# Value weights' raws and query tables in free ring tiles, two weight splits behind the exponentials, latents' splits in other heads

## The chip, the cores and the metric

The kernel runs on one core of a Trainium2 chip. The time is the device time of one execution in microseconds (us); of several executions the median is given. Everything is computed in 32-bit floating point; a matrix product is made of three passes (high part by high part, high by low, low by high) over operands that are split into a rounded high part and a rest.

## The reference, cut to what matters

One denoising step of a two-layer backbone on 512 latent tokens and 128 prompt tokens, with 128 cached tokens. The even layer joins 8 heads of latent attention (MLA) and 8 heads of neighbourhood attention; the change touches the end of the neighbourhood heads and the start of the MLA heads.

```python
def even_mixer_latent(h, c_ckv, c_krope, c_nk, c_nv, w_in, q_norm, w_uq, kv_norm, w_ukv, rpb, w_out, cos, sin):
    q, ckv, krope, nq, nk, nv = even_project(h, w_in, q_norm, w_uq, kv_norm, w_ukv)
    q = jnp.concatenate([q[..., :MLA_NOPE_DIM], apply_rope(q[..., MLA_NOPE_DIM:], cos, sin)], axis=-1)
    krope = apply_rope(krope[:, :, None, :], cos, sin)[:, :, 0, :]
    k_lat, v_lat = mla_expand(ckv, w_ukv, krope)
    k_ctx, v_ctx = mla_expand(c_ckv, w_ukv, c_krope)
    a_mla = attend_blocked(q, jnp.concatenate([k_lat, k_ctx], axis=1),
                           jnp.concatenate([v_lat, v_ctx], axis=1), MLA_SCALE)
    a_na = neighbourhood_attention(nq, nk, nv, c_nk, c_nv, rpb)
    return jnp.concatenate([a_mla.reshape(b, L, -1), a_na.reshape(b, L, -1)], axis=-1) @ w_out
```

## The kernel before, in words

The order of each engine's instructions is fixed when the program is built: the code names pieces of TensorE's work in strings (`NA_ORDER`, L963, for the neighbourhood heads 0 to 7), `sequence` (L121) runs them in that order, and a scheduler places the instructions of the other engines; `after(inst, fn)` and `issue_after` put what `fn` issues on an engine behind `inst` on that engine. Every engine works through its own instructions in order, so one that waits holds all behind it. SyncE (SP) issues nearly all DMAs, in order too.

In the heads, `s` are scores, `t` transposes of the probabilities, `v` products with values, `q` the next pair's query or key projection, `m` modulation products, `sp`, `pt`, `pv` the prompt's part, and `pk` the place of a split of latents. Of the scores (`ns`), VectorE (DVE) adds the bias and takes the extreme (`np`, `nm`, the ISA rows), ScalarE (ACT) takes the exponential, GpSimd (POOL) scales it. Transposes (`nt`) are split into `nts_..h` by a copy of ACT and `nts_..l` by a subtraction of DVE, and then multiply the values into `no`. Score banks in PSUM come from a pool `y` of four.

`unit` (L170) loads a weight tile into one of three raw buffers (`rawp`), and splits it by a copy of ACT and a subtraction of DVE or POOL. `wna` (L709) does so for the query and key weights of the neighbourhood heads, pair by pair: `wnq2` and `wnq3` are the query weights of pairs 2 and 3, split one pair ahead. `split_in_place` (L863) splits the compressed latents `ckv`, `cq`, `kr`, `cc` in place, one entry of `SPLIT_AT` (L878) in each of heads 0 to 5, behind that head's second exponential. `moved` and `latents` (L883, L893) copy low parts and prompt columns into ring tiles by DMA (`ckv0l`, `ckph`, `ckpl`, `cq0l`). The ring holds eight tiles of each of the tags `x`, `hh` and `hl`; when head 6 begins its end, the eight `hh` tiles with the high parts of the layer's input have had their last reader.

Behind head 6's pieces the code takes the first MLA weights `wm0` (L1002), the latents, key tiles `kT`, and the value weights `wmv` (L1008). `k_pieces` and `q_pieces` (L930, L944) make MLA keys and queries; a query is multiplied by a rotation table `tq`, which head 7 loads for MLA head 0 into a raw buffer, and which is loaded again for all heads, two rows, when the neighbourhood pool is closed (L1030).

Of the kernel before, what the change touches and what calls it, by code (L numbers as in the profile page):

```python
# [51 lines left out]
def body(ctx, tc, xT, vecs, crow, wm0, wm0g1, wm0g, wm1, wA, wNV, wNA, wMK, wMV, wOA, wGQ, wGK, wGV, wOC,  # L52
# [53 lines left out]
    def f(ap):  # L106
        return ap.bitcast(F32)
# [62 lines left out]
    def unit(src, n, name, lo="v", pool=None, bufs=3):  # L170

        raw = load(src, n, name + "r")
        t = (pool or wp).tile([P, 2, 1024], F32R, tag="w", bufs=bufs, name=name)
        hi, lw = t[:, 0, :n], t[:, 1, :n]
        S.activation(hi, raw, AF.Copy)
        (V if lo == "v" else G).tensor_tensor(lw, raw, f(hi), ALU.subtract)
        return hi, lw
# [538 lines left out]

# [120 lines left out]

    wmk, nexps = {}, {}  # L840
# [32 lines left out]
    def cached_latents():  # L873
# [1 line left out]
        nc.sync.dma_start(cc, cckvT.rearrange("u p n -> p u n"))  # L875
        split_in_place("cc", cc, [("u", 0, 256)])
    HALVES = [("u", 0, HT), ("u", HT, T)]
    SPLIT_AT = [lambda: split_in_place("ckv0", ckv[0], [("t", 0, T)]),  # L878
                lambda: split_in_place("ckv1", ckv[1], [("t", 0, T)]), lambda: split_in_place("cq0", cq[0], HALVES),
                lambda: split_in_place("cq1", cq[1], HALVES), lambda: split_in_place("kr", kr, [("t", 0, T), ("u", T, 768)]),  # L880
                cached_latents]

    def moved(name):  # L883

# [82 lines left out]
    for h in range(8):  # L967
        p, r = divmod(h, 2)
        if r == 0:
            oN.append(ring.tile([P, T], F32, tag="x", name=f"oN{p}"))  # L970
            pfirst, psecond = prompt_pair([nv[4][:, 2 * p + i, :] for i in range(2)], oN[p], ab, f"npp{p}",
                                         lambda name: bank(name, "y"))
        pts = []
        sc = na_scores(h, bm, pts)
        if h < 7:
            bm = na_bias(h + 1)
        qh, ql, ks = [t[r] for t in nqk[p]]
        pieces = named("s", sc)
        if h < 6:
            pieces["pk"] = lambda h=h: after(nexps[h, 1], SPLIT_AT[h])  # L980

        def prompt_scores(pss, qh=qh, ql=ql, ks=ks):
            PE.matmul(pss, qh[:, NS:T], ks[:, 896:1024], start=True, stop=False)
            PE.matmul(pss, ql[:, NS:T], ks[:, 896:1024], start=False, stop=True)
        pieces["sp"] = pfirst(r, prompt_scores)
        if p < 3:
            pieces.update(named("q", na_q(p + 1) if r == 0 else na_k(p + 1)))
        for n, at in enumerate(M_AT):
            if h == at:
                pieces.update(named("n" if "m0" in pieces else "m", mod0(4 + n, lambda n=n: bank(f"mod{4 + n}", "y"),  # L990
                                                                               mod_raw_w if h == 6 else mod_raw)))
        if h == 7:
            cql = after(fetched["wmvr"], lambda: [moved(f"cq{u}") for u in range(2)])
            pieces.update(k_pieces(0, ybank))
            pieces.update(named("u", q_pieces(0, ybank, lambda c: ring.tile([P, T], F32R, tag="h" + c, name=f"mq{c}0"),
                                              lazy(lambda: load(tabM[:, 0, :], T, "tq0")))))
        sequence(NA_ORDER[h] if h else "q0 q1 s0 m0 q2 s1 sp pk q3 q4 q5 m1 q6 q7 m2", {**pieces, **tail})
        tail = na_values(h, pts, oN[p])
        if r == 1:
            tail.update(psecond)  # L1000
        if h == 6:
            mla_w(0)  # L1002
            lat = latents()
            kT = [[ring.tile([P, T], F32R, tag="h" + c, name=f"kT{c}{r}") for r in range(2)] for c in "hl"]
            kTp = ring.tile([P, T], F32R, tag="x", name="kTp")
            even_keys, first_odd = [[(kT[i][r], kTp[:, P * (2 * i + r):P * (2 * i + r + 1)]) for i in range(2)] for r in range(2)]
            odd_keys = [first_odd]
            wmv = unit(wMV, 1024, "wmv")  # L1008
        if h == 7:
            with tc.issue_after(fetched["cq1"].ins):  # L1010
                for r in range(2):
                    k_rope(r, (slice(64, 128), slice(0, 64))[r])
# [14 lines left out]

    sb = ExitStack()
    cp = sb.enter_context(tc.tile_pool(name="cp", bufs=1, reuse_waits="tile"))
    tq = cp.tile([P, 2, T], F32, name="tq")  # L1030
    nc.sync.dma_start(tq, tabM)
    mv = [cp.tile([P, 8, P], F32R, name=f"mv{i}") for i in range(6)]
    odd_keys.append([(cp.tile([P, T], F32R, name=f"kTo{c}"), cp.tile([P, P], F32R, name=f"kTq{c}")) for c in "hl"])
    k_rope(1, slice(0, 64), 1)
# [1130 lines left out]
```

## Time and profile before

| | us |
|---|---|
| median of 3 executions (lowest, highest) | 1475.03 (1474.27, 1476.35) |
| the profiled execution | 1473.69 |
| its span, from the first to the last instruction | 1471.9 |
| TensorE matmuls busy in it | 1437.1 |
| granted TensorE clock, mean | 0.999 |
| neighbourhood heads 0 to 7 | about 110 to 221 of the span |

The engines are PE (TensorE), DVE, ACT, POOL and SP; the profile's lines name an engine, the line of the kernel, the operation, and the tile written and those read. An idle time in brackets is that of the engine ahead of the instruction, with what ended it.

### The profile page before, as it was taken

How to read it: one execution, taken by the hardware profiler on the slowest of the kernel's cores; microseconds unless marked ns; L12 is line 12 of the kernel's file. 1: busy time of each engine (PE TensorE's matmuls, PEld its weight loads, DVE VectorE, ACT ScalarE, POOL GpSimd, SP SyncE). 2: the span in 40 equal slices, each digit the busy share in tenths (PEclk: the TensorE clock that was granted, in tenths of full speed). 3: DMA queues.
4: the chain of work that ended last, by engine and by line, in shares of the span. 5: the costliest groups of instructions: out<-in, count | busy, mean ns of one | idle time of the engine just before them, and what ended most of it. 6: DMA issues, size and time to landing. Idle time of an engine off the chain costs nothing.

```text
span 1471.9 us, 25844 instructions
## 1 busy us (share of the span) xinstructions
PE 1437.1 (98%) x9764; PEld 1387.6 (94%) x9764; DVE 1230.3 (84%) x2352; ACT 781.3 (53%) x1530; POOL 177.2 (12%) x276
## 2 busy tenths in 40 slices
PE   5999999999999999999999999999999999999997
PEld 3988888889999999999999999989999999999997
DVE  5876768977998888965997888888899898989976
ACT  5446667763755555531223656672656555555443
POOL 0046645520000000000000122220000000000000
PEclk9999999999999999999999999999999999999999
DMA  9643451125165555568764311115245555548572
GB/s 371 220 155 122 135 168 58 43 82 191 47 219 171 169 169 170 169 241 313 239 223 145 98 33 30 46 49 179 87 167 190 179 178 182 176 142 294 186 267 72
DMA packets 82581, 234.50 MB, mean 159 GB/s; under 512 B 9241, under 2 KB 15545, under 8 KB 82073
## 3 DMA queue, kind: packets, MB, share of 16 engines
q1 hardware_dynamic: 80096, 228.44, 46.3%
q10 hardware_dynamic: 1944, 3.48, 0.7%
q8 instruction: 76, 1.25, 0.4%
q0 software_dynamic: 416, 0.93, 0.2%
q14 instruction: 49, 0.39, 0.1%
HBM read 193.15 MB, written 36.66 MB: 156 GB/s over the span
## 4 chain that ended last, share of the span: by engine, by line
PE 87%; DVE 5%; DMA 3%; ACT 3%; issue 2%; POOL 0%; DVEq 0%; SPq 0%; ACTq 0%
PE fg L64 21%; PE fd L64 9%; PE fgo L64 5%; PE fo L64 5%; PE fu L64 4%; PE gq L64 3%; PE fdo L64 2%; PE nk L64 2%; PE gs L64 2%; PE go L64 2%; PE nq L64 1%; PE fuo L64 1%; DMA mraw<-in_wm 1%; PE gt L68 1%; PE gvp L64 1%
## 5 line engine op out<-in xcount | busy, mean ns | idle before, releaser
L1732 DVE SCALAR_TENSOR_TENSOR junk<-wm,cb 128x1024 bf16<-128x1024 f32 x88 | 107.4, 1220 | 5.7 <-DMA wm<-in_wm 5.0
L64 PE MATMUL gq<-h10h,wgq 128*128 128x320 f32 x256 | 65.8, 316 | 0.0
L269 POOL TENSOR_SCALAR h10h<-h10t,gs,mods 128x320 fp32r<-128x320 f32 x4 | 3.9, 990 | 429.8 <-DVE h10t L263 427.5
L1472 ACT ACTIVATE wY<-s 128x1024 fp32r<-128x1024 f32 x38 | 40.3, 1060 | 26.6 <-PE fg L64 22.6
L2000 POOL TENSOR_TENSOR xr<-xw,fn1rs 128x320 f32<-128x320 f32 x2 | 1.7, 866 | 412.9 <-ACT fn1rs L237 412.9
L1472 ACT ACTIVATE wZ<-s 128x1024 fp32r<-128x1024 f32 x38 | 40.2, 1057 | 19.7 <-PE fd L64 15.4
L1473 DVE TENSOR_TENSOR wZ<-s,wZ 128x1024 fp32r<-128x1024 f32 x38 | 46.5, 1223 | 2.2
L1473 DVE TENSOR_TENSOR wY<-s,wY 128x1024 fp32r<-128x1024 f32 x38 | 46.4, 1220 | 0.2
L64 PEld LDWEIGHTS gq<-h10h,wgq 128*128 128x128 f32 x256 | 44.9, 189 | 0.6
L1581 DVE TENSOR_TENSOR sg<-up,sg 128x640 f32<-128x640 f32 x38 | 31.3, 823 | 15.7 <-ACT sg L1580 14.6
L1580 ACT ACTIVATE sg<-fg 128x320 f32<-128x320 f32 x38 | 16.7, 439 | 48.0 <-PE fg L64 48.0
L1602 ACT ACTIVATE p<-fd 128x320 f32<-128x320 f32 x38 | 16.6, 438 | 46.3 <-PE fd L64 46.3
L64 PE MATMUL gq<-h10l,wgq 128*128 128x320 f32 x128 | 39.5, 308 | 0.0
L1937 ACT ACTIVATE gp<-gs,gb,rq 128x640 f32<-128x640 f32 (+1 forms) x40 | 31.8, 796 | 13.2 <-DVE gb L1936 11.8
L64 PE MATMUL fg<-h01E,wW 128*128 128x320 f32 x228 | 36.7, 310 | 1.1 <-DVE g L1612 1.1
L64 PE MATMUL fg<-h11N,wZ 128*128 128x320 f32 x228 | 36.7, 309 | 0.0
L64 PE MATMUL fg<-h01q,wX 128*128 128x320 f32 x228 | 36.7, 309 | 0.0
L64 PE MATMUL fu<-h11q,wX 128*128 128x320 f32 x228 | 36.6, 309 | 0.0
L64 PE MATMUL fd<-h01q,wZ 128*128 128x320 f32 x228 | 36.6, 309 | 0.0
L64 PE MATMUL fd<-h11q,wZ 128*128 128x320 f32 x228 | 36.6, 309 | 0.0
L64 PE MATMUL fg<-h11q,wX 128*128 128x320 f32 x228 | 36.5, 309 | 0.0
L64 PE MATMUL fg<-h11E,wW 128*128 128x320 f32 x228 | 36.5, 309 | 0.0
(3412 smaller groups left out, 5289.1 us busy)
## 6 DMA issues: line engine op xcount, KB each, us to landing
wm<-in_wm SPq DMA_DIRECT2D x48, 512.0 KB, 4.2
mraw<-in_wm SPq DMA_DIRECT2D x8, 1024.0 KB, 13.2
mraw<-in_wm SPq DMA_DIRECT2D x14, 512.0 KB, 4.4
wmv<-in_wm0g SPq DMA_DIRECT2D x8, 512.0 KB, 3.8
wm<-in_wm0g SPq DMA_DIRECT2D x8, 512.0 KB, 4.8
ruo<-in_wFO SPq DMA_DIRECT2D x8, 512.0 KB, 4.3
rgo<-in_wFO SPq DMA_DIRECT2D x8, 512.0 KB, 5.4
x<-in_xT SPq DMA_DIRECT2D x8, 320.0 KB, 5.3
```

The source lines that it names most:

```text
L64: cls.last = nc.tensor.matmul(*a, **k)
L68: cls.last = nc.tensor.transpose(*a, **k)
L269: G.tensor_scalar(h[:, c0:c1], t, self.gsl[:, k, 0:1], self.ml[:, self.sh + k, 0:1], ALU.mult, ALU.add)
L1472: S.activation(h, src, AF.Copy)
L1473: V.tensor_tensor(w_, src, f(h), ALU.subtract)
L1580: last = S.activation(sg[:, 0:HT], g[:, :HT], AF.Silu, scale=-1.0)
L1581: V.tensor_tensor(sg, up, sg, ALU.mult)
L1602: S.activation(p5, b5[:, :HT], AF.Copy)
L1732: V.scalar_tensor_tensor(junk, raw, 1.0, cb[:, c, :], ALU.mult, ALU.mult, accum_out=mods[l][:, j0 + i, c:c + 1])
L1937: gexp[h, j] = S.activation(dst, src, AF.Exp, bias=nb, scale=rq[:, j:j + 1], accum_out=ll[:, j:j + 1])
L2000: G.tensor_tensor(x[k][:, c0:c1], root[1][k], nrm.rs[:, c0:c1], ALU.mult)
```

## The change

- `wna` issues a weight split behind the last exponential of an earlier head, where that exponential has been issued: `wnq2` behind head 0's, `wnq3` behind head 2's.
- `SPLIT_AT` has four places in place of six: head 0 splits `ckv0`, head 1 `ckv1` and `cq0`, head 3 `cq1` and `kr`, head 5 `cc`.
- The raws of `wmv` are loaded in two halves into two `hh` ring tiles, behind the load of `wm0` and ahead of the latents' copies, and split in halves. Before, they went into a raw buffer behind these copies.
- Both rows of the rotation table are loaded into two more `hh` tiles behind the latents' copies. Head 7's own load of one row and the later load of two rows are gone.

```diff
         for p_, i_ in ((p, i), (p + i, 1 - i)):
             if p_ < 4 and (p_, i_) not in wnas:
-                wnas[p_, i_] = unit(wNA[p_, i_], 1024, f"wn{'qk'[i_]}{p_}")
+                wnas[p_, i_] = after(nexps.get((2 * p + i - 3, 3)), lambda: unit(wNA[p_, i_], 1024, f"wn{'qk'[i_]}{p_}"))
...
-    SPLIT_AT = [lambda: split_in_place("ckv0", ckv[0], [("t", 0, T)]),
-                lambda: split_in_place("ckv1", ckv[1], [("t", 0, T)]), lambda: split_in_place("cq0", cq[0], HALVES),
-                lambda: split_in_place("cq1", cq[1], HALVES), lambda: split_in_place("kr", kr, [("t", 0, T), ("u", T, 768)]),
-                cached_latents]
+    SPLIT_AT = {0: lambda: split_in_place("ckv0", ckv[0], [("t", 0, T)]),
+                1: lambda: (split_in_place("ckv1", ckv[1], [("t", 0, T)]), split_in_place("cq0", cq[0], HALVES)),
+                3: lambda: (split_in_place("cq1", cq[1], HALVES), split_in_place("kr", kr, [("t", 0, T), ("u", T, 768)])),
+                5: cached_latents}
...
-            cql = after(fetched["wmvr"], lambda: [moved(f"cq{u}") for u in range(2)])
+            cql = after(fetched["tq"], lambda: [moved(f"cq{u}") for u in range(2)])
...
-                                              lazy(lambda: load(tabM[:, 0, :], T, "tq0")))))
+                                              lambda: f(tq[0]))))
...
-            lat = latents()
...
-            wmv = unit(wMV, 1024, "wmv")
+            wmvr = [ring.tile([P, T], F32R, tag="hh", name=f"wmvr{u}") for u in range(2)]
+            tq = [ring.tile([P, T], F32R, tag="hh", name=f"tq{r}") for r in range(2)]
+            with tc.issue_after(fetched["wm0r"].ins):
+                for u in range(2):
+                    fetched["wmvr"] = nc.sync.dma_start(f(wmvr[u][:, :512]), wMV[:, 512 * u:512 * u + 512])
+                lat = latents()
+                for r in range(2):
+                    fetched["tq"] = nc.sync.dma_start(f(tq[r]), tabM[:, r, :])
+            wmv = wp.tile([P, 2, 1024], F32R, tag="w", bufs=3, name="wmv")
+            for u in range(2):
+                c = slice(512 * u, 512 * u + 512)
+                S.activation(wmv[:, 0, c], f(wmvr[u][:, :512]), AF.Copy)
+                V.tensor_tensor(wmv[:, 1, c], f(wmvr[u][:, :512]), f(wmv[:, 0, c]), ALU.subtract)
+            wmv = wmv[:, 0, :], wmv[:, 1, :]
...
-    tq = cp.tile([P, 2, T], F32, name="tq")
-    nc.sync.dma_start(tq, tabM)
```

TensorE's order is the same in both programs. Three places where the others differ follow; a row is line, operation, the tile written and those read, and its shape.

ACT in head 2, from the half sum of head 1's output (`nhs`) on, before:

```order
L418 ACTIVATE nhs_1517<-no_1420 64x512
L175 ACTIVATE wnq_1740<-wnq3r 128x1024
L405 ACTIVATE nts_0h<-nt_0_1571 128x512
L802 ACTIVATE np_0_1552,nl_1528<-np_0_1552,nm_1527 128x384
L802 ACTIVATE np_1_1558,nl_1528<-np_1_1558,nm_1527 128x384
L405 ACTIVATE nts_1h<-nt_1_1580 128x512
L869 ACTIVATE hicq_1631<-cqr_594 128x320
L869 ACTIVATE hicq_1634<-cqr_594 128x320
L802 ACTIVATE np_2_1607,nl_1528<-np_2_1607,nm_1527 128x384
L802 ACTIVATE np_3_1613,nl_1528<-np_3_1613,nm_1527 128x384
L405 ACTIVATE nts_2h<-nt_2_1622 128x512
L728 ACTIVATE nqh_1542<-nq_1564 64x64
```

and in the change:

```order
L418 ACTIVATE nhs_1523<-no_1420 64x512
L405 ACTIVATE nts_0h<-nt_0_1577 128x512
L802 ACTIVATE np_0_1558,nl_1534<-np_0_1558,nm_1533 128x384
L802 ACTIVATE np_1_1564,nl_1534<-np_1_1564,nm_1533 128x384
L405 ACTIVATE nts_1h<-nt_1_1586 128x512
L802 ACTIVATE np_2_1613,nl_1534<-np_2_1613,nm_1533 128x384
L802 ACTIVATE np_3_1619,nl_1534<-np_3_1619,nm_1533 128x384
L405 ACTIVATE nts_2h<-nt_2_1628 128x512
L728 ACTIVATE nqh_1548<-nq_1570 64x64
L175 ACTIVATE wnq_1740<-wnq3r 128x1024
L728 ACTIVATE nqh_1549<-nq_1570 64x64
```

The copy of `wnq3r` stood ahead of `nts_0h` and all exponentials, and stands behind head 2's first query copy `nqh` now; the two rows of `hicq` have gone to head 1.

SP between head 6 and head 7, from `ckv0l` to the last part of `ckpl`, before:

```order
L889 DMA ckv0l<-ckvr_748 128x640
L889 DMA ckv1l<-ckvr_753 128x640
L901 DMA ckph<-hickv_1263 128x128
L901 DMA ckph<-hickv_1432 128x128
L902 DMA ckph<-hicc_2254 128x2x128
L167 DMA wmvr<-in_wMV 128x1024
L889 DMA cq0l<-cqr_594 128x320 x2
L889 DMA cq1l<-cqr_599 128x320 x2
L167 DMA tq_2648<-in_tabM 128x640
L901 DMA ckpl<-ckvr_748 128x128
L901 DMA ckpl<-ckvr_753 128x128
L902 DMA ckpl<-cc 128x2x128
```

and in the change, where the two loads of `wmvr` stand directly behind `wm0r` and ahead of `ckv0l`:

```order
L889 DMA ckv1l<-ckvr_753 128x640
L901 DMA ckph<-hickv_1263 128x128
L901 DMA ckph<-hickv_1432 128x128
L902 DMA ckph<-hicc_2254 128x2x128
L1014 DMA tq_2507<-in_tabM 128x640
L1014 DMA tq_2508<-in_tabM 128x640
L889 DMA cq0l<-cqr_594 128x320 x2
L889 DMA cq1l<-cqr_599 128x320 x2
L927 DMA kTh_2500<-hikr_1849 64x640
L901 DMA ckpl<-ckvr_748 128x128
L901 DMA ckpl<-ckvr_753 128x128
L902 DMA ckpl<-cc 128x2x128
```

Two loads of `tq` stand ahead of the copies of `cq0` and `cq1`, where one stood behind them, and one row of `kTh` has come ahead of `ckpl`.

DVE at the same place, from the last of head 6's transposes to head 7's first scores, before:

```order
L409 TENSOR_TENSOR nts_2l<-nt_2_2436,nts_2h 128x512
L396 RECIPROCAL nr_2r<-nl_2350 128x1
L445 TENSOR_REDUCE npp3m_2448<-npp3s_2445 128x1
L396 RECIPROCAL nr_3r<-nl_2350 128x1
L396 RECIPROCAL npp3r0r<-npp3l_2450 128x1
L381 TENSOR_TENSOR mods_98<-mod_2420,vec 128x4 x2
L475 TENSOR_TENSOR oN_1939<-npp2o,npp2h 64x128 x2
L800 ISA np_0_2538,nm_2522<-ns_00_2532,bm_1004 128x384
L800 ISA nm_2522 128x1
L800 ISA np_1_2544,nm_2522<-ns_01_2533,bm_1004 128x384
L800 ISA nm_2522 128x1
L176 TENSOR_TENSOR wmv<-wmvr,wmv 128x1024
```

and in the change:

```order
L409 TENSOR_TENSOR nts_2l<-nt_2_2436,nts_2h 128x512
L396 RECIPROCAL nr_2r<-nl_2350 128x1
L445 TENSOR_REDUCE npp3m_2448<-npp3s_2445 128x1
L1019 TENSOR_TENSOR wmv<-wmvr_2505,wmv 128x512
L396 RECIPROCAL nr_3r<-nl_2350 128x1
L396 RECIPROCAL npp3r0r<-npp3l_2450 128x1
L1019 TENSOR_TENSOR wmv<-wmvr_2506,wmv 128x512
L381 TENSOR_TENSOR mods_98<-mod_2420,vec 128x4
L475 TENSOR_TENSOR oN_1945<-npp2o,npp2h 64x128 x2
L381 TENSOR_TENSOR mods_98<-mod_2420,vec 128x4
L800 ISA np_0_2546,nm_2530<-ns_00_2540,bm_1004 128x384
```

The subtraction of `wmv`, one row behind head 7's first two score passes before, is in two halves ahead of them now, the second ahead of `mods`. On ACT the halves' copies stand in the same way: the first directly behind the copy of `wm0r` and ahead of `nts_2h`, the second behind `npp3p`.

More of the change, by code (lines that the diff above doesn't have):

```diff
@@ L706, in body @@
     qbanks = [qbank, lambda name: bank(name, "y")]
-    nqk, wnas, done_with = {}, {}, {}
+    nqk, wnas, done_with, nexps = {}, {}, {}, {}
     def wna(p, i):
@@ L836, in na_values @@
         return {**{f"t{n}": trs(n) for n in range(3)}, **{f"v{n}": av(n) for n in range(3)}}
-    wmk, nexps = {}, {}
+    wmk = {}
     def mla_w(p):
@@ L978, in body @@
         pieces = named("s", sc)
-        if h < 6:
+        if h in SPLIT_AT:
             pieces["pk"] = lambda h=h: after(nexps[h, 1], SPLIT_AT[h])
@@ L1039, in mla_q @@
     def mla_q(h):
-        return q_pieces(h, qbank, lambda c: cp.tile([P, T], F32R, tag=f"mq{c}", bufs=2, name=f"mq{c}{h}"), lambda: tq[:, h % 2, :])
+        return q_pieces(h, qbank, lambda c: cp.tile([P, T], F32R, tag=f"mq{c}", bufs=2, name=f"mq{c}{h}"), lambda: f(tq[h % 2]))
     def mla_scores(h, pts, beside):
```

## The prediction

> **What bounds the kernel now.** The page comes first, for the engine that carries the span, then the busy time of each engine by stage, then the order in time of PE, ACT, DVE and SP inside the stages that show idle PE.
>
> ```profile
> span 1471.9 us, 25844 instructions
> PE 1437.1 (98%) x9764; PEld 1387.6 (94%) x9764; DVE 1230.3 (84%) x2352; ACT 781.3 (53%) x1530; POOL 177.2 (12%) x276
> 133.00:149.00 16.00, 13.54 (x90) 12.16 (x89) 10.38 (x32) 9.36 (x25) 8.36 (x18) 1.00 0.51 166
> 199.60:210.60 11.00, 9.06 (x61) 8.04 (x60) 9.65 (x30) 8.39 (x22) 2.94 (x6) 1.00 0.70 186
> 220.90:235.30 14.40, 12.63 (x79) 11.16 (x77) 9.30 (x22) 8.60 (x20) 5.55 (x8) 1.00 0.37 108
> ```
>
> PE is busy 98% of the span, so only idle PE can be won, or a new idle time lost. In the windows (stretch, its length, then busy PE, PEld, DVE, ACT, POOL, granted clock, DMA share, GB/s) head 2 lacks 2.46 us of PE, head 7 lacks 1.94, the first MLA heads lack 1.77. The clock is 1.00 in all three. The change removes no matmul and leaves PE's order as it was, so everything it can do is to shift PE's waits in 110 to 240 us.
>
> **Head 2.** Rows in order of time: start, length, engine, line, operation, and in brackets the idle time before it.
>
> ```profile
> 138.12 0.34 PE L64 MATMUL ns<-nk,nql 128*128 128x384 f32 x1
> 139.60 0.49 PE L64 MATMUL no<-nts_0h,nv 128*128 128x512 f32 x1 [1.13 <-ACT nts_0h L405]
> 140.32 0.50 PE L64 MATMUL no<-nts_0l,nv 128*128 128x512 f32 x1 [0.23 <-DVE nts_0l L409]
> 145.32 0.50 PE L64 MATMUL no<-nts_2l,nv 128*128 128x256 f32 x2 [0.22 <-DVE nts_2l L409]
> 147.49 0.31 PE L64 MATMUL nq<-h00h,wnq 128*128 128x320 f32 x1
> 148.61 0.33 PE L64 MATMUL npp0o<-npp0pth,nv 128*128 128x128 f32 x1 [0.81 <-ACT npp0pth L405]
> 149.15 0.33 PE L64 MATMUL npp0o<-npp0ptl,nv 128*128 128x128 f32 x1 [0.21 <-DVE npp0ptl L409]
> 168.88 0.33 PE L64 MATMUL ns<-nk,nql 128*128 128x384 f32 x1
> 169.06 0.39 PE L64 MATMUL no<-nts_0h,nv 128*128 128x512 f32 x1
> 169.29 0.39 PE L64 MATMUL no<-nts_0l,nv 128*128 128x512 f32 x1
> ```
>
> The last three rows are the same pair in head 4, where nothing waits: the starts lie 0.18 and 0.23 us apart. In head 2 they lie 1.48 and 0.72 apart, so 1.30 + 0.49 = 1.79 us are lost there. The printed idle times are smaller, since ends are modelled; I count by starts. At 145.32 I take the printed 0.22. Before the prompt's product, 1.12 and 0.54 against 0.18 each lose 0.94 + 0.36 = 1.30. Head 2 loses 3.31 us in all.
>
> ```profile
> 137.86 1.06 ACT L175 ACTIVATE wnq<-wnq3r 128x1024 fp32r<-128x1024 f32 x1 [3.95 <-DMA wnq3r<-in_wNA]
> 141.12 0.82 ACT L869 ACTIVATE hicq<-cqr 128x320 fp32r<-128x320 f32 x2
> 144.44 0.21 ACT L728 ACTIVATE nqh<-nq 64x64 fp32r<-64x64 f32 x1
> 148.18 0.37 ACT L405 ACTIVATE npp0pth<-npp0t 128x256 fp32r<-128x256 f32 x1
> 140.32 1.21 DVE L176 TENSOR_TENSOR wnq<-wnq3r,wnq 128x1024 fp32r<-128x1024 f32 x1
> ```
>
> ACT stood 3.95 us on the load of wnq3r with the copy nts_0h queued behind it. Now that copy and the exponentials go first. PE's transposes for nts_0h are over by 135.8, so its copy ends near 136.1, two us ahead of the use: the 1.79 goes, and so does the 0.22 at nts_2l, since ACT no longer runs the 1.06 and the 0.82 (the cq0 split, gone to head 1) ahead of it. What is late next is the prompt's npp0pth. Its ACT chain (nqh, nql and so on in turn) can start some 3.5 us earlier, at about 140.95, but has wnq's 1.06 on ACT and 1.21 on DVE in it now; the chain had 1.54 us of idle, so it grows by 0.73 to 2.27. That puts npp0pth at 145.4 to 146.9, where PE, 2.01 us earlier, wants it at 145.65 and needs 0.43 from its start. Of the 1.30 us, 0.85 stays by my choice (the nearer end, as two of the chain's three idle gaps lie where wnq lands), with 0.5 and 2.1 as ends. **Head 2: 3.31 - 0.85 = 2.46 us won**, from 1.2 to 2.8.
>
> **Heads 0, 1 and 3.** wnq2's split moves from ahead of head 0's scores to behind its exponentials, into the same chain; ckv1 and cq0 share head 1, cq1 and kr share head 3. PE shows no idle time there, and what it uses next stands 0.4 to 4 us earlier in the rows of ACT and DVE. The next loads into wnq2r's and wnq3r's buffers (mraw, for modulation products some 10 us later) are covered by that distance. I take 0; if the cover is gone (the tightest place is the bank that np_2 gives up in heads 1 and 3), 0.5 us is lost.
>
> **Heads 6 and 7.**
>
> ```profile
> 195.61 0.84 ACT L175 ACTIVATE wm<-wm0r 128x768 fp32r<-128x768 f32 x1
> 198.07 0.37 ACT L373 ACTIVATE modsb<-mod 128x256 f32<-128x256 f32 x1
> 200.92 1.06 ACT L175 ACTIVATE wmv<-wmvr 128x1024 fp32r<-128x1024 f32 x1 [1.71 <-DMA wmvr<-in_wMV]
> 198.63 0.56 PE L64 MATMUL mod<-sel,modsb 128*128 128x4 f32 x4
> 203.05 0.40 PE L64 MATMUL mk<-hickv,wm 128*128 128x512 f32 x1
> 204.34 0.50 PE L64 MATMUL no<-nts_0h,nv 128*128 128x512 f32 x1 [0.90 <-ACT nts_0h L405]
> 205.88 0.50 PE L64 MATMUL no<-nts_0l,nv 128*128 128x512 f32 x1 [1.04 <-DVE nts_0l L409]
> 207.00 0.28 PE L64 MATMUL mk<-ckpl,wm 128*128 128x256 f32 x1
> 205.13 0.69 DVE L409 TENSOR_TENSOR nts_0l<-nt,nts_0h 128x512 fp32r<-128x512 f32 x1
> ```
>
> 1.29 and 1.54 against 0.23 each: 1.06 + 1.31 = 2.37 us lost, because ACT stood on wmvr. Now the two halves load right behind wm0r. But the first half's copy (half of 1.06, about 0.53) stands ahead of nts_2h, np_2, np_3 and modsb on ACT: modsb had 0.19 us in hand (198.07 + 0.37 to 198.63), so PE waits about 0.35 there. The second half's subtraction stands on DVE ahead of mods and of head 7's first score pass, which I put near 201.4, so PE waits about 0.45 for the bank that mods gives up, and nts_0l, behind four score passes, starts at 204.3 instead of 205.13. Net, PE passes 205.88 some 0.85 us earlier.
>
> Then the transfers:
>
> ```profile
> 198.52 0.60 SPq L889 DMA_DIRECT2D cq1l<-cqr  x1
> cq1l<-cqr SPq DMA_DIRECT2D x1, 160.0 KB, 4.0
> 199.22 0.54 SPq L167 DMA_DIRECT2D tq<-in_tabM  x1
> tq<-in_tabM SPq DMA_DIRECT2D x1, 320.0 KB, 4.1
> 201.76 1.11 SPq L901 DMA_DIRECT2D ckpl<-ckvr  x2
> 202.96 0.63 SPq L902 DMA_DIRECT2D ckpl<-cc  x1
> ckpl<-cc SPq DMA_DIRECT2D x1, 128.0 KB, 2.2
> ```
>
> ckpl goes into the buffer that cq0 leaves, so it is issued when the copies of cq0 have landed (SP stands still until 201.76). Its last part landed at 202.96 + 2.2 = 205.2, 1.8 us ahead of its use at 207.00. In the change both tables stand ahead of cq0's copies. One table takes 0.8 us of the queue (cq1l landed at 202.5, the table behind it at 203.3), two take 1.6, so ckpl lands near 206.8, and PE, which would be there at 207.00 - 0.85 = 206.15, waits for it. **0.2 us won**; the ends are 2.37 (no new wait) and -1.0.
>
> In the Trainium skill, "DMA: Bandwidth & Descriptors", section "Queues, rings and completion order", each DMA engine takes the descriptors of one ring in order, and all that SP issues is on one row of rings. By that rule a load put ahead delays every copy behind it, as the landings of cq1l and tq agree; were it otherwise, the term would be 0.85 in place of 0.2.
>
> **The first MLA heads.**
>
> ```profile
> 226.85 0.39 PE L64 MATMUL mv<-wmv,ckpl 128*128 128x512 f32 x1
> 228.45 0.56 PE L64 MATMUL ms<-kTh,mqh 128*128 128x320 f32 x2 [1.21 <-ACT mp L1059]
> 235.31 0.41 PE L64 MATMUL mq<-hicq,wm 128*128 128x320 f32 x1 [0.44 <-DVE mqt L950]
> 226.25 0.49 DVE L950 TENSOR_TENSOR mqt<-mq,tq 128x320 f32<-128x320 f32 x1 [3.02 <-DMA tq<-in_tabM]
> ```
>
> DVE stood 3.02 us on the table; the next maximum, the exponential and the score bank were behind it. The table now lies in the ring long before, so mqt runs near 223.2 and the exponential that frees the bank ends near 225.5, ahead of PE at 227.1: 1.60 - 0.23 = 1.37 goes. With DVE 3 us ahead, I take 0.3 of the 0.44 at 235.31 as well. **1.67 us won**, from 1.37 to 1.81. The load of two rows at 220.3 goes too, and nothing on PE stood behind it but this.
>
> **The sum.** 2.46 + 0 + 0.2 + 1.67 = 4.33, say 4.4 us. The profiled execution took 1473.69 us, 1.8 beyond its span, so it would be 1469.3; it lies 1.34 below the median of the runs, 1475.03, which is the time compared: 1475.03 - 4.4 = **1470.6 us**.
>
> **The rivals.**
>
> *All waits go*: the transfers keep up and the chain in head 2 hides wnq. 3.31 + 2.37 + 1.81 = 7.5 us, 1467.5. For it speaks that ACT is busy only 53%; against it, ACT and DVE take turns in the chain, and the tables are in the queue.
>
> *The waits come back in place*: wnq's split keeps npp0pth at its late end (head 2 wins 1.2), and head 7 gives back what it wins (0). With 1.37 for MLA that is 2.6 us, 1472.4, within the bound. For it speaks the chain's growth of up to 2.27.
>
> *The loads do no good*: were a tile of the ring taken only later, wmvr would wait for it as it waited for its place before, and head 7 gains nothing; 2.46 + 1.67 = 4.1, hardly another time, so it is no case of its own.
>
> *Slower*: wmv's first half stands on ACT ahead of head 6's last two exponentials. wm0r had landed by 195.61, and the half must be there at 196.4. Each us that it lands later holds ACT, head 6's values and head 7's transposes by the same us. At 200.8 the sum is 0; from about 203.8 the change is slower by more than 3 us, some 1478. Against it speaks that the halves stand directly behind wm0r in SP's order.
>
> **How the numbers follow.** Forecast 0.47, all waits go 0.22 (also the values between), waits come back 0.22, slower 0.09. The range goes from all waits gone, 1467.0, to the waits that come back with the 0.5 us of heads 0, 1 and 3 and the runs' own spread, 1474.3. A measurement tells about 0.2%, 2.95 us, from no change: the forecast and the first rival lie beyond it, the second just within. Faster 0.70, same 0.23, slower 0.07.
>
> **What would show it.** In the changed profile: nts_0h in head 2 ahead of wnq's copy and PE without a wait at v0; a wait of some 0.85 left at npp0pth; in head 7 a PE wait named modsb, a smaller one at nts_0l and one named ckpl; no wait of DVE on tq in the first MLA head. A ckpl that lands by 205 would lift the sum towards 1469; an ACT wait on wmvr above 0.5 us would break the forecast, and a PE wait in heads 1 or 3 would show the cover at zero cost to be wrong.

## The result and the profile after

The change takes 1471.02 us, the median of 17 executions (1469.56 to 1474.2); before takes 1475.03 on the same chip (17 executions, 1473.24 to 1477.37). The ratio is 0.9976, 95% interval 0.9968 to 0.9983: 4.0 us between the medians, 2.5 to 4.7 by the interval. The profiled execution of the change took 1473.53 us, one of its longer ones; its own profile shows why, as follows below. First its page and the three windows of before (stretch, length, busy PE, PEld, DVE, ACT, POOL, granted clock, DMA share, GB/s):

```profile
span 1471.2 us, 25849 instructions
PE 1438.7 (98%) x9764; PEld 1391.0 (95%) x9764; DVE 1232.6 (84%) x2353; ACT 781.5 (53%) x1531; POOL 178.5 (12%) x276
133.00:149.00 16.00, 14.70 (x104) 14.15 (x105) 12.32 (x37) 9.92 (x28) 7.55 (x18) 1.00 0.45 154
199.60:210.60 11.00, 8.53 (x44) 7.64 (x43) 7.42 (x25) 6.30 (x19) 2.73 (x5) 0.77 0.54 130
220.90:235.30 14.40, 14.29 (x89) 13.19 (x88) 11.77 (x25) 10.08 (x24) 6.74 (x9) 1.00 0.25 64
```

PE lacks 1.30 us in head 2's window instead of 2.46 and 0.11 in the first MLA heads' instead of 1.77. In head 7's it lacks 2.47 instead of 1.94, and the clock there is 0.77. The windows are fixed in time, while the work in them has moved by up to 2.4 us; the table below goes by the work.

Head 2 in order of time (start, length, engine, line, operation, idle time before it):

```profile
138.07 0.39 PE L64 MATMUL no<-nts_0h,nv 128*128 128x512 f32 x1
138.30 0.39 PE L64 MATMUL no<-nts_0l,nv 128*128 128x512 f32 x1
140.80 1.05 ACT L175 ACTIVATE wnq<-wnq3r 128x1024 fp32r<-128x1024 f32 x1
141.88 1.53 DVE L176 TENSOR_TENSOR wnq<-wnq3r,wnq 128x1024 fp32r<-128x1024 f32 x1 [0.24 <-ACT wnq L175]
144.82 0.31 PE L64 MATMUL nq<-h00h,wnq 128*128 128x320 f32 x1
145.49 0.37 ACT L405 ACTIVATE npp0pth<-npp0t 128x256 fp32r<-128x256 f32 x1
145.91 0.33 PE L64 MATMUL npp0o<-npp0pth,nv 128*128 128x128 f32 x1 [0.79 <-ACT npp0pth L405]
146.28 0.42 DVE L409 TENSOR_TENSOR npp0ptl<-npp0t,npp0pth 128x256 fp32r<-128x256 f32 x1
146.76 0.33 PE L64 MATMUL npp0o<-npp0ptl,nv 128*128 128x128 f32 x1 [0.52 <-DVE npp0ptl L409]
147.14 0.39 PE L64 MATMUL ns<-nk,nqh 128*128 128x384 f32 x1
```

`nts_0h` and `nts_0l` are ready now (the starts lie 0.23 us apart, as in heads without a wait). The wait at the prompt's product has not shrunk: against 0.18 each, 1.09 and 0.85 between the starts lose 0.91 + 0.67 = 1.58 us, where the kernel before lost 1.30. wnq's copy and subtraction stand in the chain ahead of it, and the subtraction takes 1.53 us, not 1.21.

Heads 6 and 7, PE, then SP's issues of the same stretch:

```profile
196.39 0.61 PE L64 MATMUL mod<-sel,modsb 128*128 128x4 f32 x4
199.00 0.41 PE L64 MATMUL ns<-nk,nqh 128*128 128x384 f32 x1 [0.37 <-DVE mods L381]
202.43 0.50 PE L64 MATMUL no<-nts_0l,nv 128*128 128x512 f32 x1 [0.35 <-DVE nts_0l L409]
203.38 0.34 PE L64 MATMUL mk<-ckph,wm 128*128 128x256 f32 x1
205.83 0.55 PE L64 MATMUL mk<-ckpl,wm 128*128 128x256 f32 x1 [2.11 <-DMA ckpl<-cc]
```

```profile
188.20 0.37 SPq L167 DMA_DIRECT2D wm0r<-in_wMK  x1
193.71 1.24 SPq L1014 DMA_DIRECT2D tq<-in_tabM  x2
195.07 1.38 SPq L889 DMA_DIRECT2D cq0l<-cqr  x2
202.29 1.11 SPq L901 DMA_DIRECT2D ckpl<-ckvr  x2
203.50 0.63 SPq L902 DMA_DIRECT2D ckpl<-cc  x1
```

What head 7 lost at `nts_0h` and `nts_0l` before is nearly gone (0.35 left), and one wait of 2.11 us for `ckpl` stands in its place: from the load of wm0 to the issue of ckpl SP takes 14.1 us (202.29 - 188.20), and took 11.2 before (201.76 - 190.59). Behind that wait the granted clock is halved (windows as above):

```profile
205.00:213.00 8.00, 7.17 (x33) 7.16 (x34) 3.45 (x10) 2.27 (x8) 1.24 (x2) 0.57 0.77 216
213.00:218.00 5.00, 5.00 (x33) 4.37 (x31) 2.50 (x5) 2.32 (x5) 0.88 (x1) 1.00 0.09 35
```

In the first MLA heads the score pass that waited 1.21 us and the query projection that waited 0.44 start without a wait:

```profile
228.74 0.39 PE L64 MATMUL mv<-wmv,ckpl 128*128 128x512 f32 x1
228.97 0.45 PE L64 MATMUL ms<-kTh,mqh 128*128 128x320 f32 x2
235.01 0.41 PE L64 MATMUL mq<-hicq,wm 128*128 128x320 f32 x1
```

### One table for all profiles

PE does the same work in the same order in every version here, so a matmul's start minus its start in the profile of before tells what was won up to it. The table gives, after the forecast's line, the us won between such marks: the first `ns` of heads 0, 1, 2 and 3, `npp2o<-npp2pth` (head 6), the first `mk<-ckpl`, the last `mv<-wmv,ckpl` of the first MLA head, the next `mk<-ckpl`. For example, the change loses 1.22 up to ckpl: it stands 2.39 ahead at npp2o (195.85 for 198.24) and 1.17 ahead at ckpl (205.83 for 207.00). Where nothing differs, head 2 repeats within 0.15 us from profile to profile and the first MLA heads within 0.35, but in heads 6 and 7 before's own two profiles lie 0.60 apart.

| profile | head 0 | head 1 | head 2 | heads 6, 7 to ckpl | ckpl to MLA (clock) | first MLA heads | sum |
|---|---|---|---|---|---|---|---|
| forecast | 0 | 0 | 2.46 | 0.2 | 0 | 1.67 | 4.33 |
| before again (e11) | 0.01 | 0 | -0.15 | 0.60 | 0 | -0.08 | 0.40 |
| the change | 0.37 | 0 | 2.16 | -1.22 | -3.06 | 2.15 | 0.40 |
| the change again (e7) | 0.37 | -0.30 | 2.16 | -1.10 | -0.08 | 2.16 | 3.21 |
| weights alone (e1) | 0.37 | -0.18 | 2.23 | 0.48 | 0 | -0.28 | 2.63 |
| without the ring part (e2) | 0.37 | -0.11 | 2.16 | 0.07 | -0.02 | -0.34 | 2.14 |
| ring part alone (e3) | 0.01 | 0 | 0.96 | 0 | -0.07 | 2.16 | 3.09 |
| tables behind ckpl (e4) | 0.37 | -0.29 | 2.16 | 1.07 | -0.02 | 2.15 | 5.44 |
| wnq3 later (e6) | 0.38 | -0.50 | 3.32 | -1.12 | -1.64 | 2.15 | 2.66 |
| both (e8) | 0.37 | -0.40 | 3.32 | 0.36 | -0.01 | 2.15 | 5.85 |
| tables on another queue (e9) | 0.37 | -0.34 | 2.17 | -0.77 | -0.07 | 2.15 | 3.51 |
| cq1's copies first (e10) | 0.37 | -0.30 | 2.15 | -1.22 | -0.08 | 2.16 | 3.08 |
| both, wmv later too (e12) | 0.37 | -0.02 | 3.31 | 1.21 | -0.07 | 2.15 | 7.01 |
| ckpl much later (e13) | 0.37 | -0.03 | 2.15 | -5.73 | -2.31 | 2.16 | -3.39 |

Heads 3 to 5 win 0 to 0.07, which is in the sum alone.

### The profile page after: what moved, and what is told of

Same layout as the page of the kernel before. It is cut to its first block, busy times and chain, and to the rows that moved or that the text cites. A ratio compares the mean times of both kernels' runs of the same rounds, so it can differ in the third digit from the quotient of the medians.

```text
span 1471.2 us, 25849 instructions
## 1 busy us (share of the span) xinstructions
PE 1438.7 (98%) x9764; PEld 1391.0 (95%) x9764; DVE 1232.6 (84%) x2353; ACT 781.5 (53%) x1531; POOL 178.5 (12%) x276
## 4 chain that ended last, share of the span: by engine, by line
PE 88%; DVE 5%; ACT 3%; DMA 2%; issue 2%; SPq 0%; DVEq 0%; ACTq 0%
PE fg L64 21%; PE fd L64 9%; PE fgo L64 5%; PE fo L64 5%; PE fu L64 4%; PE gq L64 3%; PE fdo L64 2%; PE nk L64 2%; PE gs L64 2%; PE go L64 2%; PE nq L64 1%; PE fuo L64 1%; PE gt L68 1%; PE mod L64 1%; PE gvp L64 1%
## 5 line engine op out<-in xcount | busy, mean ns | idle before, releaser
L64 PE MATMUL fg<-h01N,wZ 128*128 128x320 f32 x228 | 36.6, 309 | 0.0
```

The lines of the kernel that those rows point to most:

```text
L64: cls.last = nc.tensor.matmul(*a, **k)
```

## The experiments

The theory that the runs test: head 2 and the MLA heads win as the steps said, head 7 loses by ckpl, which the tables ahead of it in SP's order make late, and PE's long idle time at ckpl can halve the clock. Each time stands beside runs of before on the same chip.

### Which part brings what: e1, e2, e3

e1 is the kernel before with one line of the change, e2 is the change with the hunks on `wmvr` and `tq` undone, e3 has these hunks alone.

```diff
-                wnas[p_, i_] = unit(wNA[p_, i_], 1024, f"wn{'qk'[i_]}{p_}")
+                wnas[p_, i_] = after(nexps.get((2 * p + i - 3, 3)), lambda: unit(wNA[p_, i_], 1024, f"wn{'qk'[i_]}{p_}"))
```

> Only the neighbourhood weights' splits are moved behind the exponentials; latents' splits and the ring's loads stand as before. Theory (head 2's waits come from the copy that stood on the load of wnq3r): PE's waits at nts_0h and nts_0l in head 2 go, some 1.0 to 1.3 us stay at npp0pth and npp0ptl, heads 0 to 2 win 2.2 to 2.6 us, about 1472.5 us; heads 6 and 7 and the first MLA heads as before (idle 0.90 and 1.04 us at nts_0h and nts_0l of head 7). Rival (half of it comes from cq0's split leaving head 2): a wait at nts_2l of 0.2 us or more and a larger one at npp0pth stay, under 1.5 us won, about 1473.7 us.

> The change without the loads to ring tiles (weights' splits and latents' splits moved, value weights' raws and tables as before). Theory: the same 2.2 to 2.6 us as the weights alone (latents' splits are worth 0 plus or minus 0.3), so about 1472.5 us, 1.0 to 2.0 us above the whole change; PE waits of 0.90 and 1.04 us in head 7 and 1.21 and 0.44 us in the first MLA heads as before, granted clock 1.00 from 205 to 213 us. Rival (the ring part loses as much as it wins, by the wait at ckpl and the halved clock behind it): as fast as the whole change, 1470 to 1471 us.

> Only the loads to ring tiles (value weights' halves and both tables); weights' and latents' splits stand as before. Theory (the ring part wins 2.2 us in the first MLA heads and gives back 1.1 to 1.2 in head 7, where the wait at ckpl takes the place of those at nts_0h and nts_0l, and the whole change's win is the sum of its parts): PE's waits in head 2 as before, a wait at mk<-ckpl of 1.3 to 2.1 us, no wait at mp and mqt in the first MLA heads, about 1 us faster, 1474 to 1474.5 us beside some 1475.3 before. Rival 1 (PE comes 2.4 us later and SP does not, so ckpl is there in time): wait at ckpl below 0.5 us, 2.5 us or more faster. Rival 2 (the halved clock behind the wait eats the rest): same as before or slower, 1475.3 us or more.

Measured: e1 1471.33 us, ratio 0.9971 (0.9960 to 0.9982); e2 1472.15, 0.9971 (0.9961 to 0.9981), both beside 1475.84 for before; e3 1473.20 beside 1474.14, 0.9993 (0.9985 to 1.0002). By the table the weights win 2.2 us in head 2 whether cq0's split leaves it or not, so e1's rival falls, and the latents' splits are worth nothing that can be told apart (the 0.41 between e1 and e2 in head 7 is no more than the 0.60 between before's own two profiles there, e11). The ring part wins 2.16 in the MLA heads in every profile that has it, and loses nothing in head 7 when it stands alone, but 1.1 to 1.2 when the weights' part is there too. The runs show less of it than the profiles: e3 cannot be told from before, and by the ratios the whole change (0.9976, and 0.9978 in e7) is not ahead of e1 and e2, which leave the ring part out. So e2's rival, that the ring part loses as much as it wins, is not refuted by the times. e3's rows in head 7:

```profile
198.92 0.61 PE L64 MATMUL mod<-sel,modsb 128*128 128x4 f32 x4 [0.18 <-ACT modsb L373]
201.50 0.41 PE L64 MATMUL ns<-nk,nqh 128*128 128x384 f32 x1 [0.35 <-DVE mods L381]
204.94 0.50 PE L64 MATMUL no<-nts_0l,nv 128*128 128x512 f32 x1 [0.35 <-DVE nts_0l L409]
206.95 0.35 PE L64 MATMUL mk<-ckpl,wm 128*128 128x256 f32 x1 [0.72 <-DMA ckpl<-cc]
```

```profile
190.53 0.37 SPq L167 DMA_DIRECT2D wm0r<-in_wMK  x1
203.41 1.11 SPq L901 DMA_DIRECT2D ckpl<-ckvr  x2
```

Here are the four waits of the forecast (`modsb`, `mods`, `nts_0l`, `ckpl`), with ckpl's at 0.72 us: from wm0 to ckpl SP takes 12.9 us, 1.7 more than before. The expected 1.3 to 2.1 at ckpl was wrong, and so was rival 1's "below 0.5". e3's 0.96 in head 2 is no work of the ring part: its first scores started 0.95 us later than before's, and ACT's wait for wnq3r, 3.95 us before, was shorter by as much:

```profile
137.84 1.06 ACT L175 ACTIVATE wnq<-wnq3r 128x1024 fp32r<-128x1024 f32 x1 [2.98 <-DMA wnq3r<-in_wNA]
```

### What makes ckpl late: e4, e9, e10

```diff
+                    fetched[f"ckp{c}"] = nc.sync.dma_start(n3[:, :, 0:P], f(parts["cc"][0][c]).rearrange("p (u n) -> p u n", u=2))
...
-                for r in range(2):
-                    fetched["tq"] = nc.sync.dma_start(f(tq[r]), tabM[:, r, :])
...
-            cql = after(fetched["tq"], lambda: [moved(f"cq{u}") for u in range(2)])
+            cql = after(fetched["wmvr"], lambda: [moved(f"cq{u}") for u in range(2)])
+            with tc.issue_after(fetched["ckp1"].ins):
+                for r in range(2):
+                    nc.sync.dma_start(f(tq[r]), tabM[:, r, :])
```

> The change with the two table loads issued behind ckpl's in SP's order, and not ahead of cq0's copies. Theory (the tables ahead of cq0's copies make ckpl late, and the idle time of 2.11 us at ckpl sets off the halved clock): ckpl lands 1.4 us or more earlier, PE's wait at mk<-ckpl falls below 0.7 us, granted clock 1.00 from 205 to 213 us, the profiled span 4 to 5 us shorter than the change's 1471.2, the median 1467 to 1469.5 us. Rival 1 (ckpl is late by the value weights' halves or by cq0's own copies): the wait stays at 1.5 us or more, 1470 to 1471.5 us. Rival 2 (the clock drops there whatever the wait): wait gone, but granted clock near 0.5 still stands somewhere from 200 to 215 us.

Measured: 1469.02 us beside 1475.84, ratio 0.9955 (0.9940 to 0.9969). PE has no wait at ckpl, and head 7 wins 1.07 where the change loses 1.22. The clock is 1.00:

```profile
205.00:213.00 8.00, 8.00 (x56) 7.34 (x54) 6.17 (x16) 4.94 (x14) 2.18 (x4) 1.00 0.87 256
```

The loads stand behind ckpl and still nobody waits for them: the first MLA heads win the same 2.15. So in heads 6 and 7 the tables ahead of cq0's copies cost 2.3 us (1.07 + 1.22), and brought nothing by being there; from wm0 to ckpl's issue SP takes 11.3 us here. e9 issues them where the change does, but by GpSimd on its own queue (`nc.gpsimd.dma_start`, and cq's copies again behind `wmvr`).

> The change with the two table loads issued by GpSimd on its own queue, and the latents' copies directly behind ckph's on SP's. Theory (SP's queue works in order, and what stands ahead in it delays cq0's copies): ckpl lands 1.4 us or more earlier against its use, PE's wait there is below 0.7 us, as with the tables behind ckpl, about 1469 us. Rival (it is the bytes, which all queues share): the wait stays at 1.3 us or more, about 1471 us.

Measured: 1472.15 us beside 1475.57, ratio 0.9977 (0.9968 to 0.9986). The wait at ckpl is gone, but only because PE comes later (in the last line the granted clock stands behind the busy times):

```profile
195.48 0.63 ACT L1018 ACTIVATE wmv<-wmvr 128x512 fp32r<-128x512 f32 x1 [1.34 <-DMA wmvr<-in_wMV]
198.11 0.61 PE L64 MATMUL mod<-sel,modsb 128*128 128x4 f32 x4 [1.45 <-ACT modsb L373]
202.12 1.11 SPq L901 DMA_DIRECT2D ckpl<-ckvr  x2
199.00:200.00 1.00, 1.00 (x5) 1.00 (x5) 1.00 (x3) 0.33 (x1) 1.00 (x2) 0.50 1.04 373
```

ckpl is issued at 202.12, as in the change at 202.29 (13.7 us behind wm0's load, for 14.1), though the tables are not in SP's queue: it is the bytes, which the queues share. The Trainium skill, "DMA: Bandwidth & Descriptors", section "Issuing engines are not separate DMA queues", says the same: DMAs of different issuing engines end on the same 16 DMA engines and interleave; these rows agree.

Worse, the tables now run beside wmv's first half, ACT waits 1.34 us for it with modsb behind, and PE waits 1.45. This is the mechanism of the forecast's slower rival, at a smaller price. Behind that wait the clock is halved from 198.8 to 202.2 us, so a part of the 0.77 that heads 6 and 7 lose here is the clock's.

e10 exchanges the order of the copies of cq0 and cq1 (the second hunk keeps the `k_rope` loads behind whichever copy is last).

```diff
-            cql = after(fetched["tq"], lambda: [moved(f"cq{u}") for u in range(2)])
+            cql = after(fetched["tq"], lambda: [moved(f"cq{u}") for u in (1, 0)][::-1])
...
-            with tc.issue_after(fetched["cq1"].ins):
+            with tc.issue_after(fetched["cq0"].ins):
```

> The change with the copies of cq1 issued ahead of those of cq0. Theory (ckpl takes the buffer that cq0 leaves, so its issue waits for cq0's copies): ckpl is issued 0.8 to 2 us later, PE's wait at it grows from 2.1 to 2.9 us or more, the granted clock falls to 0.50 behind it, the median 1472 to 1474 us. Rival (cq1's copies or the order on SP gate it): the wait is 2.1 us or less, about 1471 us.

Measured: 1472.29 us beside 1475.57, ratio 0.9978 (0.9969 to 0.9988); the wait is 1.38 us, where 2.9 or more was expected. In the waits of SP's queue, ckpl's issue now waits for cq1's copies:

```profile
SPq L901 <- DMA cq1l<-cqr: 2.7, 1, 2.7
```

ckpl takes the buffer that the first pair of copies leaves, whichever that is.

### The halved clock: e7, e13, e11

> The change itself once more, beside its variants. Theory: the wait at mk<-ckpl is there in every execution, 1.8 to 2.3 us (SP's order and PE's are fixed), and the median is 1470.5 to 1471.5 us. Whether the granted clock is halved behind it is open: if the wait sets it off, it is near 0.50 for 3 us or more within 204 to 214 us again; if such drops fall anywhere, it is 1.00 there and the span is about 3 us shorter than 1471.2.

Measured: 1471.77 us beside 1475.57, ratio 0.9978 (0.9969 to 0.9987). The same program waits 1.35 us at ckpl this time, not the expected 1.8 to 2.3, and the clock stays at 1.00 behind it, so its sum in the table is 2.8 us above that of the change's first profile. ckpl is issued at 202.25, for 202.29 in the first profile; it is PE that comes later, since ACT waits 0.55 us for wmv's first half and PE 0.65 us for modsb behind it. ACT's and PE's rows, then the window:

```profile
194.49 0.63 ACT L1018 ACTIVATE wmv<-wmvr 128x512 fp32r<-128x512 f32 x1 [0.55 <-DMA wmvr<-in_wMV]
205.78 0.36 PE L64 MATMUL mk<-ckpl,wm 128*128 128x256 f32 x1 [1.35 <-DMA ckpl<-cc]
```

```profile
205.00:213.00 8.00, 7.21 (x50) 6.82 (x51) 6.13 (x15) 4.72 (x13) 2.12 (x3) 1.00 0.78 216
```

e13 lengthens the wait: ckpl's three loads are taken out of `latents` and go behind the eight `k_rope` loads.

```diff
...
+            with tc.issue_after(fetched["kr"].ins):
+                n3 = f(fetched["near"][1][:, :512]).rearrange("p (u n) -> p u n", u=2)
+                for u in range(2):
+                    nc.sync.dma_start(n3[:, u, P:], f(parts[f"ckv{u}"][0][1][:, NS:T]))
+                nc.sync.dma_start(n3[:, :, 0:P], f(parts["cc"][0][1]).rearrange("p (u n) -> p u n", u=2))
```

> The change with ckpl's three loads behind the eight loads of the rotary keys in SP's order, so that PE stands idle at mk<-ckpl some 5 to 7 us in place of 1.3 to 2.1. Theory (a long idle time of PE sets off the halved clock): granted clock near 0.50 for 3 us or more right behind the wait in the profile, and a median longer by the added wait and 2 to 3.5 us more, some 1478 us, mean clock of most runs 0.996 or less. Rival (the drop is no matter of the idle time): clock 1.00 behind the wait, a median longer by the added wait alone, some 1475.5 us.

Measured: 1477.44 us beside 1475.03, ratio 1.0015 (1.0005 to 1.0025). Again PE's row and the window behind it:

```profile
209.83 0.55 PE L64 MATMUL mk<-ckpl,wm 128*128 128x256 f32 x1 [6.09 <-DMA ckpl<-cc]
```

```profile
209.00:216.00 7.00, 6.17 (x31) 6.19 (x32) 1.83 (x6) 1.82 (x6) 0.00 (x0) 0.59 0.54 178
```

A wait of 6.09 us is followed by the halved clock, which costs 2.31 us more, and the mean clock of all ten executions is 0.996 or less (5 of 11 in e7, 3 of 17 of the change, 0 of 15 in e4, e8 and e12). So the theory holds for the long wait. For the shorter ones the mean clock proves nothing, since 39 of 74 executions of before, which has no wait at ckpl, are at 0.996 or less too; what the traces show of them stands in the last section.

> The kernel before once more, for a second profiled execution. Its first took 1473.69 us at a mean granted clock of 0.999, while the 42 runs beside the variants so far have a mean clock of 0.9965 and some 1475.9 us. Theory (halved clock falls in places of low PE use, in before as well): a stretch of 3 us or more near 0.50 stands ahead of the span's last 10 us in this profile too, and the span is above 1473 us. Rival (before has none, the runs differ for another reason): granted clock 1.00 throughout, span 1471.9 plus or minus 0.5.

Measured: 1474.05 us, span 1472.3 (above 1473 was expected), and at the program's start:

```profile
22.00:28.00 6.00, 5.01 (x35) 3.74 (x36) 5.29 (x13) 4.30 (x9) 0.00 (x0) 0.72 1.03 410
```

Before has such stretches too (its first profile has none until the span's end). Of the fourteen profiles here, six have one between 22 and 30 us (e2, e3, e4, e10, e11, e12), two one near 861 us (e1, e7), four one in heads 6 and 7 (the change, e6, e9, e13), and before's first and e8 none until the end. In the six, head 0's first scores start 0.5 to 1.7 us later than in before's first profile, which the table does not hold; in the others they are 0.4 us off at most. Over 74 executions of before beside e1 to e13 the mean clock is 0.9966, and the time goes with it: 1473.77 us on average at 0.998 (16 executions), 1475.87 at 0.996 (25).

### What is left, and the best version: e6, e8, e12

e6 puts wnq3's split behind the prompt's copy; e8 is e6 with e4's order of the tables.

```diff
-        S.activation(shape(h), ps, AF.Copy)
+        fetched[name] = S.activation(shape(h), ps, AF.Copy)
...
-                wnas[p_, i_] = after(nexps.get((2 * p + i - 3, 3)), lambda: unit(wNA[p_, i_], 1024, f"wn{'qk'[i_]}{p_}"))
+                wnas[p_, i_] = after(fetched["npp0pt"] if (p, i) == (2, 1) else nexps.get((2 * p + i - 3, 3)), lambda: unit(wNA[p_, i_], 1024, f"wn{'qk'[i_]}{p_}"))
```

> The change with wnq3's split behind the prompt's copy npp0pth and not inside the chain ahead of it. Theory (wnq's 1.05 us on ACT and 1.53 us on DVE delay npp0pth): PE's waits of 0.79 and 0.52 us at npp0pth and npp0ptl fall to 0.3 us together or less, head 3 starts 0.9 to 1.3 us earlier, about 1470 us. Rival (the chain moves the wait): PE waits by about the same time at head 3's first scores or transposes, whose exponentials stand behind the split; same time as the change, 1471 us.

> Both variants together: tables behind ckpl's loads, wnq3's split behind npp0pth. Theory (each stands for itself): no PE wait at npp0pth, npp0ptl and ckpl above 0.3 us, 0.8 to 1.3 us faster than the tables' variant alone, 1467.5 to 1468.3 us. Rival (what comes earlier in head 2 meets ckpl, whose landing is set by the transfers): a wait at ckpl of about 0.8 us comes back, same time as the tables' variant, about 1469 us.

Measured: e6 1470.82 us beside 1475.84, ratio 0.9965 (0.9952 to 0.9978); e8 **1467.71** beside 1475.57, **0.9949 (0.9936 to 0.9961)**. Head 2 now wins 3.32 us, all that it lost; the split behind the prompt's copy delays nobody:

```profile
145.34 0.33 PE L64 MATMUL npp0o<-npp0pth,nv 128*128 128x128 f32 x1
145.80 0.33 PE L64 MATMUL npp0o<-npp0ptl,nv 128*128 128x128 f32 x1
146.18 0.39 PE L64 MATMUL ns<-nk,nqh 128*128 128x384 f32 x1
```

In e6 that gain lasts up to ckpl (heads 6 and 7 lose 1.12, as in the change) and is lost again to 1.64 us of halved clock, behind a wait of 1.22 us there. With the tables out of the way (e8) the clock holds, but only 0.4 us of the gain is left against e4 (5.85 for 5.44): ACT now waits 0.61 us for wmv's first half, and PE 0.71 us for modsb behind it. By the ratios e8 and e4 cannot be told apart.

e12 is e8 with wmv's two halves split behind head 7's second and fourth exponentials (`issue_after(nexps[7, 1 + 2 * u].ins)`).

> Tables behind ckpl, wnq3's split behind npp0pth, and the value weights' two halves split behind head 7's exponentials instead of ahead of head 6's. Theory (the halves' copies on ACT and subtractions on DVE are what makes PE wait 0.7 us at modsb, 0.35 at mods and 0.35 at nts_0l): these three waits go, 1.0 to 1.4 us faster than without it, about 1466.5 us. Rival (the halves then delay nts_2h, k's split or the value products of the first MLA head): a wait of 0.5 us or more at one of these, same time as without it, 1467.7 us.

Measured: 1468.41 us beside 1475.03, ratio 0.9956 (0.9942 to 0.9969). The waits at modsb and mods go, 0.18 stays at nts_0l, and PE, now faster, meets ckpl again:

```profile
202.61 0.36 PE L64 MATMUL mk<-ckpl,wm 128*128 128x256 f32 x1 [0.55 <-DMA ckpl<-cc]
```

By the table e12 is 1.16 us ahead of e8; by the ratios, taken on different chips, neither is better. e8 beats both the change and before; whether e12 adds to it stays open.

## Why the prediction was right, and where it was not

The time came out at 1471.02 for 1470.6 forecast, nearer than its parts, and that is luck in part. By the table the change wins 3.2 to 3.5 us without the halved clock at ckpl (e7's 3.21; 0.40 + 3.06 in the first profile), not 4.33: heads 6 and 7 cost 1.3 to 1.4 us more than forecast, head 2 wins 0.3 less, and head 0 and the first MLA heads give 0.85 back. The 4.0 us of the runs (2.5 to 4.7) fit 3.2 to 3.5 as well as 4.33.

- **Head 2, 2.46 forecast, 2.16 measured.** The waits at `nts_0h` and `nts_0l` went (1.90 won up to the next transposes, 1.79 forecast), the one at `nts_2l` too (0.54 up to the next projection, 0.22 forecast). At `npp0pth` 1.58 us stay, not 0.85. The chain with wnq in it came out as forecast: `npp0pth` starts at 145.49, at the near end of the 145.4 to 146.9. What was off is when PE wants it: at 145.00 (144.82 + 0.18) and not at 145.65, because PE is ahead by head 0's win and the larger wins above, and it spends that lead waiting. The rest is `npp0ptl`, which loses 0.67, not 0.36. So at head 3's first scores the change is 2.39 us ahead (147.14 for 149.53), which is nearly the 2.46. e6 shows the cause by taking wnq out of the chain: both waits go.
- **Heads 0 and 1, forecast 0.** Head 0 wins 0.37 in every profile with the weights' part: its second score pass and the prompt's scores start 0.06 to 0.18 us apart now, 0.17 to 0.28 before. Head 1 loses 0 to 0.5 from profile to profile, at a key projection near 126.3 us; in e6, which loses most, PE waits 0.18 us there for DVE's `nm`. The forecast had 0.5 as the price there if the cover is gone.
- **Heads 6 and 7, forecast +0.2, measured -1.2 and -1.1.** The mechanism was right: the waits at mods, `nts_0l` and ckpl came. modsb's is too short to be named in the change's first profile (the starts lie 0.26 us apart instead of 0.11) and is 0.65 in e7, where ACT waits 0.55 us on wmvr. What was mis-sized is the step "ckpl lands near 206.8", 1.6 us for the two tables: from wm0 to ckpl's issue they add 1.7 us in e3, but 2.9 in the change (2.8 against e4, which differs in the tables' place alone). SP did keep step with PE up to wm0, whose load is issued 2.39 us earlier than before (188.20 for 190.59); behind it the transfers take 1.2 us longer than in e3. The same 3.9 MB pass between the two issues, at 278 GB/s in the change and at 302 in e3. Why was not settled.
- **First MLA heads, 1.67 forecast, 2.15 measured.** The wait at 235.31 went whole, with what its longer spacing hid.
- **The halved clock was in no term.** It costs the change 3.06 us in one profile and nothing at that place in the other. It is also in before's runs, whose median lies above its clean profile (1475.03 for 1473.69). That the shorter idle times of the change make such stretches rarer fits the mean clocks (0.9966 for before, 0.9971 over 28 runs of the change). At about 1 us for 0.001 in before's runs (1475.87 and 1473.77 above) that would be some 0.5 us, an estimate; it is not shown apart from the waits.

Of the rivals, "the waits come back" was half right (head 2's price at npp0pth, head 7's loss), "all waits go" is what e8 and e12 come near to once their cause is moved, and the slower one came in small: ACT has no wait on wmvr in the change's first profile, but 0.55 us in e7, 0.44 to 0.70 in e6, e8, e10 and e13, and 1.34 in e9. The forecast had named 0.5 us there as a sign against it; the lateness only takes the place of waiting at ckpl, and heads 6 and 7 lose 1.1 to 1.2 us with it (e6, e7, e10) and without (the change).

## What to carry to other kernels

A load that is moved ahead of others delays the transfers behind it, here even when it is issued on another queue; place it by the latest time at which it is used, here behind ckpl. When an earlier stage gets faster, reckon the next stage's transfers again: here their first issue moved with PE, by 2.39 us, but they then took 1.2 us longer. A split that is moved out of one chain should be followed to the end of the chain that it lands in, and the engine that waits there reckoned with everything it has won on the way.

## What the runs showed of the hardware that was not expected

- TensorE's granted clock falls to 0.50 behind short idle times, 2.11 us in the change, 1.22 in e6 and 1.45 in e9 (at modsb), while 1.35 in e7 and 1.38 in e10 had no such fall. Worked out from windows of 1 us, with the clock as 0.50 or 1.00, it lasts 6.8 us in the change (205.6 to 212.4) and 3.4 us in e6 (205.3 to 208.7). The Trainium skill, "TensorE: Matmul & The Clock Gate", section "Part 1: The HAM clock gate", has a free-running window of about 3.4 us and a throttle after one idle window. One and two windows fit the lengths; that a whole idle window is needed does not fit. The traces' clock records have these lengths as 3.413 and 6.827 us. Cut into steps of 3.413 us from each profile's own fall of the clock, the profiles show what differs: how much of one step PE is idle. The last step ahead of the fall in the change and in e6, then the step in e7 that holds most of its wait:

```profile
202.19:205.61 3.42, 1.28 (x8) 1.01 (x8) 3.23 (x9) 2.87 (x9) 1.18 (x2) 1.00 0.30 89
201.88:205.30 3.42, 1.85 (x13) 1.53 (x13) 3.23 (x9) 3.02 (x9) 1.23 (x3) 1.00 0.38 105
201.78:205.19 3.41, 2.31 (x13) 1.52 (x11) 3.26 (x12) 3.22 (x9) 2.17 (x4) 1.00 0.28 81
```

PE is idle for 2.1 and 1.6 us in the first two and for 1.1 in e7, whose wait lies across two steps (e10: 0.9). In all fourteen profiles, up to 1455 us, the clock falls behind seven of the eight steps at full clock with 1.55 us idle or more, behind three of the thirteen with 1.36 to 1.51, and behind two of the thousands with less, near 861 us in e1 and e7. So whether a short wait halves the clock would hang on where it falls in the steps; this sorts runs made for other questions, and no run was made to test it. e1's stretch has no idle time over 0.25 us in the six us ahead of it (PE's rows, then the window). But 1.17 us there are ten products of two columns each; whether such products count as busy was not tested:

```profile
859.86 0.55 PE L64 MATMUL gs<-gkh,gql 128*128 128x320 f32 x2 [0.25 <-DVE gql L1902]
860.25 1.17 PE L64 MATMUL gr<-ones,gsq 128*128 128x2 f32 x10
```

```profile
861.00:865.00 4.00, 4.00 (x20) 4.00 (x20) 2.84 (x6) 2.43 (x6) 0.00 (x0) 0.57 0.29 117
```

- wnq3's subtraction on DVE takes 1.45 to 1.53 us in the chain behind the exponentials, and 1.21 to 1.23 ahead of them or behind the prompt's copy. What runs beside it on GpSimd goes with that. In the chain GpSimd's scaling of `np` starts first (in the change at 141.75 for 0.59 us, with the subtraction at 141.88). In the kernel before, the subtraction starts first, at 140.32, and it is GpSimd's row from 140.51 that takes 1.47 us in place of 0.59. Behind the prompt's copy (e6, e8, e12) GpSimd has no row beside it. That the one that starts first holds up the other fits all fourteen profiles; no run was made to test it.
